# Moving the first B load to ScalarE's hardware queue, beside the first A load, in a one-core matmul and logsumexp kernel

## The chip, the core and the metric

The kernel runs on one core of one Trainium2 chip. The metric is the device time of one launch in microseconds (us). Executions of one kernel differ by about 2 us, so an effect of half a microsecond needs medians and intervals. Engine names in the profile: PE is the TensorE matmul, PEld its weight load, DVE is VectorE, ACT is ScalarE, POOL is GpSimd, SP is SyncE. A trailing "q" (SPq, ACTq) is the engine's sequencer, which issues transfers.

## The reference

```python
m, k, n = 1024, 4096, 4096
def reference(a, b):                      # float32, normal random
    x = np.matmul(a, b)
    return special.logsumexp(x, axis=-1).astype(np.float32)
```

## The kernel before

A and B come from DRAM as float32 and are worked on as float16. The product over the first 512 columns of B is done plainly, while A arrives and is transposed on TensorE; later blocks use a seven-product scheme that is not touched here. In that first stage, up to about 58 us, GpSimd's software queue brings 128x512 tiles of A and pairs of B rows, and casts them in the transfer. Only the very first tile of A (raw_a, 256 KB) and the first pair of B rows (raw_b, 512 KB) come as float32 by a hardware queue, and are cast by engines, because that queue starts earlier (first packets at 1.76 us, the software queue's at 3.97, in before's trace).

```python
    # ScalarE's activation tables, first thing in the program      [cut: set_id]
    nc.scalar.add_instruction(mybir.InstLoadActFuncSet(...))
    ...
    zeros = s5[:, KP - 1].rearrange("p q c -> p (q c)")
    nc.vector.memset(zeros[:, 0:FD], 0.0)
    warm(6)                               # six useless matmuls, to raise TensorE's clock
    coming = list(arrivals)

    def first(k0, kn, what, x):
        if what == "a":
            raw = fix_pool.tile([P, FD], f32, name="raw_a", tag="e")
            ...
            nc.sync.dma_start(out=raw, in_=a_m[x, :, k0 * P : (k0 + kn) * P])
            nc.vector.tensor_copy(out=slot, in_=raw)
            stg[k0, x] = slot
        else:
            raw = fix_pool.tile([P, 2, FD], f32, name="raw_b", tag="s")
            nc.sync.dma_start(out=raw, in_=b_rows[:, 0, :, 0:FD])
            nc.vector.tensor_copy(out=blk0.raw[0][:, 0, 0], in_=raw[:, 0])
            nc.scalar.copy(out=blk0.raw[0][:, 0, 1], in_=raw[:, 1])

    def load(k0, kn, what, x):            # loads run ahead by up to 12 tiles
        if len(coming) >= len(arrivals) - 2:
            first(k0, kn, what, x)
        elif what == "a":
            load_a(k0, kn, x)             # nc.gpsimd.dma_start
        else:
            blk0.load(k0 // 2, k0 // 2 + 1)   # nc.gpsimd.dma_start
        ...
    for n, (k0, kn, what, x) in enumerate(arrivals):
        ...
        if what == "a":
            transpose_group(k0, kn, x)    # 4 transposes, then one copy out of PSUM
        if k0 < KN and x < 3:
            warm(1)
        ...                               # the products of what has arrived
```

GpSimd's transfers use eight semaphores in turn, so its ninth transfer waits until its first has landed, and so on.

## Time and profile before

| | before |
|---|---|
| median of 6 runs | 421.9 us (421.21 to 423.07) |
| span in the profiled run | 420.3 us |
| first real matmul starts at | 5.96 us |
| TensorE busy, 15.5 to 82 us | 66.43 of 66.50 us |

From the profile's page, the chain of work that ended last, by engine:

```profile
PE 97%; DMA 1%; DVE 0%; ACT 0%; issue 0%; SPq 0%; ACTq 0%
```

The start is in the timeline. Columns: start and length in us, engine, line, operation, output and inputs, count; in brackets, how long the engine had been idle and what ended that.

```profile
0.74 1.28 ACT L56 ACT_TABLE_LOAD   x1 [0.74 <-PEq L592]
0.75 0.39 SPq L295 DMA_DIRECT2D raw_a<-in_a_dram  x1
1.20 2.74 PE L282 MATMUL acc_1_96<-s_73 128*128 128x512 f16 x6 [1.20 <-DVE s_73 L285]
1.20 0.41 SPq L300 DMA_DIRECT2D raw_b<-in_b_dram  x1
3.46 0.52 DVE L296 CAST tb<-raw_a 128x512 f16<-128x512 f32 x1 [2.32 <-DMA raw_a<-in_a_dram]
4.04 0.61 PE L203 MATMUL tps_97<-ident,tb 128*128 128x128 f16 x4
5.07 0.52 DVE L301 CAST b_0_83<-raw_b 128x512 f16<-128x512 f32 x1 [1.09 <-DMA raw_b<-in_b_dram]
5.50 0.40 DVE L214 COPY aT<-tps_97 128x512 f16<-128x512 f16 x1
5.96 1.03 PE L221 MATMUL acc_0_91<-b_0_83,aT 128*128 128x512 f16 x2 [0.47 <-DVE aT L214]
```

SyncE issues raw_a at 0.75 and raw_b at 1.20. VectorE casts raw_a when it lands, TensorE transposes it at 4.04, and VectorE could copy the transposes out at about 4.7. It stands in line behind its cast of raw_b, though, which lands only at 5.04. So the first real matmul waits for raw_b.

The DMA view, first for the stretch from 2.5 to 4.0 us (queue: packets, MB, share of the 16 engines' time; q1 is SyncE's hardware queue), then the two issues (size, us from issue to landing):

```profile
q1 hardware_dynamic: 300, 0.58, 102.3%
...
raw_b<-in_b_dram SPq DMA_DIRECT2D x1, 512.0 KB, 3.8
raw_a<-in_a_dram SPq DMA_DIRECT2D x1, 256.0 KB, 2.7
```

A share can exceed 100%, as here. One queue keeps the 16 engines at 102% and moves 0.58 MB in 1.5 us, or 385 GB/s.

### The profile page before, as it was taken

The page shows a single profiled execution, that of the slowest core. Times are in us where ns is not written, and L with a number is a line of the kernel's source. Part 1 is how long each engine was busy: PE and PEld are TensorE (multiplying, and loading weights), DVE is VectorE, ACT ScalarE, POOL GpSimd, SP SyncE. Part 2 cuts the span into 40 slices and gives each one's busy share as a digit, 9 for nine tenths or more (in the row PEclk, how much of TensorE's full clock was granted, in tenths as well). Part 3 has the DMA queues.
Part 4 walks back from the last instruction along what each step waited for, and adds up shares of the span by engine and source line. Part 5 has one row for each costly group of instructions (what it writes and reads, how often), then busy time and mean ns, then how long its engine had stood idle before and what let it go on. Part 6 is the DMA issues. An engine that isn't in the chain of part 4 may idle for free.

```text
span 420.3 us, 8528 instructions
## 1 busy us (share of the span) xinstructions
PE 414.1 (99%) x3643; PEld 348.7 (83%) x3643; DVE 259.4 (62%) x573; ACT 109.8 (26%) x279; POOL 73.0 (17%) x115
## 2 busy tenths in 40 slices
PE   8999999999999999999999999999999999999995
PEld 3555558888888888888888888888888888888885
DVE  2567587978657783258722694336832587299855
ACT  2222240141132222122222212222221222222124
POOL 7676753001010120003000030001200030120000
PEclk9999999999999999999999999999999999999999
DMA  9999999999999299003990079400990039899000
GB/s 185 202 203 203 202 205 207 207 207 214 176 199 201 39 186 207 9 2 45 207 151 2 2 123 207 73 2 2 189 207 6 2 59 207 136 188 207 8 2 1
DMA packets 57845, 53.37 MB, mean 127 GB/s; under 512 B 10192, under 2 KB 56912, under 8 KB 57808
## 3 DMA queue, kind: packets, MB, share of 16 engines
q0 software_dynamic: 48928, 49.95, 72.1%
q1 hardware_dynamic: 8880, 2.89, 4.0%
q8 instruction: 28, 0.46, 0.4%
q14 instruction: 9, 0.07, 0.0%
HBM read 100.66 MB, written 2.10 MB: 245 GB/s over the span
## 4 chain that ended last, share of the span: by engine, by line
PE 97%; DMA 1%; DVE 0%; ACT 0%; issue 0%; SPq 0%; ACTq 0%
PE acc_1_92 L221 2%; PE acc_0_91 L221 2%; PE acc_0_93 L221 2%; PE acc_1_0_1343 L399 2%; PE acc_1_0_765 L399 2%; PE acc_2_0_3643 L399 2%; PE acc_2_0_767 L399 2%; PE acc_1_0_2435 L399 2%; PE acc_0_0_763 L399 2%; PE acc_2_0_4199 L399 2%; PE acc_3_0_3231 L399 2%; PE acc_0_0_2847 L399 2%; PE acc_3_0_1611 L399 2%; PE acc_2_0_1478 L399 2%; PE acc_0_0_3927 L399 2%; PE acc_1_0_2975 L399 2%
## 5 line engine op out<-in xcount | busy, mean ns | idle before, releaser
L399 PEld LDWEIGHTS <-aT 128*128 128x128 f16 x1856 | 181.5, 98 | 21.3
L399 PEld LDWEIGHTS <-s_71 128*128 128x128 f16 x464 | 45.3, 98 | 5.5
L399 PEld LDWEIGHTS <-s_73 128*128 128x128 f16 x464 | 45.4, 98 | 5.3
L399 PEld LDWEIGHTS <-s_72 128*128 128x128 f16 x464 | 45.4, 98 | 5.3
L221 PEld LDWEIGHTS <-aT 128*128 128x128 f16 x192 | 16.8, 99 | 15.0 <-DVE aT L214 1.6
L192 POOL DMA_DIRECT2D tb<-in_a_dram x47 | 25.4, 543 | 8.1 <-DMA tb<-in_a_dram 3.1
L203 PEld LDWEIGHTS <-tb 128*128 128x128 f16 x192 | 15.0, 99 | 12.3 <-DVE tb L296 1.0
L216 ACT COPY aT<-tps_98 128x512 f16<-128x512 f16 x24 | 14.0, 585 | 38.7 <-PE tps_98 L203 38.7
L214 DVE COPY aT<-tps_97 128x512 f16<-128x512 f16 x24 | 10.2, 424 | 19.3 <-PE tps_97 L203 19.3
L84 DVE TENSOR_TENSOR aT<-aT 128x256 f16<-128x256 f16 (+1 forms) x56 | 16.1, 342 | 0.0
L203 PE MATMUL tps_97<-ident,tb 128*128 128x128 f16 x96 | 9.5, 223 | 0.1
L81 DVE TENSOR_TENSOR s_71<-aT 128x256 f16<-128x256 f16 (+1 forms) x26 | 8.2, 315 | 2.2 <-ACT aT L216 2.2
L203 PE MATMUL tps_98<-ident,tb 128*128 128x128 f16 x96 | 9.5, 224 | 0.0
L138 POOL DMA_DIRECT2D b_0_2299<-in_b_dram x1 | 0.9, 878 | 45.9 <-PE acc_3_0_2151 L399 45.9
L138 POOL DMA_DIRECT2D b_0_3379<-in_b_dram x1 | 0.9, 878 | 45.7 <-PE acc_3_0_3231 L399 45.7
L138 POOL DMA_DIRECT2D b_0_3919<-in_b_dram x1 | 0.9, 878 | 45.1 <-PE acc_3_0_3771 L399 45.1
L138 POOL DMA_DIRECT2D b_0_2839<-in_b_dram x1 | 0.9, 887 | 44.9 <-PE acc_3_0_2691 L399 44.9
L81 DVE TENSOR_TENSOR s_73<-aT 128x256 f16<-128x256 f16 (+1 forms) x26 | 8.2, 316 | 0.0
L81 DVE TENSOR_TENSOR s_72<-aT 128x256 f16<-128x256 f16 (+1 forms) x26 | 8.2, 316 | 0.0
L138 POOL DMA_DIRECT2D aT<-in_b_dram x4 | 3.5, 897 | 21.5 <-PE acc_1_0_4055 L399 21.5
L282 PE MATMUL acc_1_96<-s_73 128*128 128x512 f16 x11 | 5.2, 609 | 1.2 <-DVE s_73 L285 1.2
L81 DVE TENSOR_TENSOR tb<-aT 128x1024 f16<-128x1024 f16 x8 | 5.2, 687 | 1.5 <-DMA aT<-in_b_dram 1.5
(1050 smaller groups left out, 893.0 us busy)
## 6 DMA issues: line engine op xcount, KB each, us to landing
tb<-in_a_dram POOLq DMA_DIRECT2D x47, 128.0 KB, 5.9
aT<-in_b_dram POOLq DMA_DIRECT2D x4, 1024.0 KB, 15.2
b_1_84<-in_b_dram POOLq DMA_DIRECT2D x4, 256.0 KB, 6.2
b_2_85<-in_b_dram POOLq DMA_DIRECT2D x4, 256.0 KB, 6.2
b_3_86<-in_b_dram POOLq DMA_DIRECT2D x4, 256.0 KB, 6.2
b_0_87<-in_b_dram POOLq DMA_DIRECT2D x2, 512.0 KB, 8.6
b_1_88<-in_b_dram POOLq DMA_DIRECT2D x2, 512.0 KB, 11.8
b_2_89<-in_b_dram POOLq DMA_DIRECT2D x2, 512.0 KB, 15.2
```

The source lines that it names most:

```text
L81: nc.vector.tensor_tensor(out=o, in0=x, in1=y, op=ALU.add)
L84: nc.vector.tensor_tensor(out=o, in0=x, in1=y, op=ALU.subtract)
L138: nc.gpsimd.dma_start(out=self.raw[lo // GI][:, lo % GI : lo % GI + hi - lo], in_=b_rows[:, lo:hi, :, ts(self.nb, FD)],)
L192: nc.gpsimd.dma_start(out=slot, in_=a_m[m, :, k0 * P : (k0 + kn) * P])
L203: nc.tensor.matmul(pst[:, ts(j, P)], src[:, ts(j, P)], ident, is_transpose=True, start=(j == 0), stop=(j == kn - 1),)
L214: nc.vector.tensor_copy(out=dst, in_=v)
L216: nc.scalar.copy(out=dst, in_=v)
L221: nc.tensor.matmul(pt, aT[:, i, kp, m // 2, m % 2, :], blk0.raw[i // GI][:, i % GI, kp, :], start=(done[m] == 0), stop=(done[m] == KT - 1),)
L282: nc.tensor.matmul(acc[2][1], zeros[:, 0:P], zeros[:, 0:FD], start=True, stop=True)
L399: nc.tensor.matmul(c, lhs(i), rhs(i), start=(start and i == 0), stop=(i == KP - 1), skip_group_check=True,)
```

## The change

raw_b is to start with raw_a instead of behind it: it goes to ScalarE's hardware queue, and its issue is put ahead of ScalarE's table load. The instruction orders of TensorE, VectorE and GpSimd are the same in both kernels.

```diff
-    tables = list(get_activation_tables(nc.m.arch).items())
-    ...
-    nc.scalar.add_instruction(mybir.InstLoadActFuncSet(...))
     ...
     warm(6)
 
+    raw_a = fix_pool.tile([P, FD], f32, name="raw_a", tag="e")
+    raw_b = fix_pool.tile([P, 2, FD], f32, name="raw_b", tag="s")
+    nc.scalar.dma_start(out=raw_b, in_=b_rows[:, 0, :, 0:FD])
+    nc.sync.dma_start(out=raw_a, in_=a_m[0, :, 0 : KN * P])
+    tables = list(get_activation_tables(nc.m.arch).items())
+    ...
+    nc.scalar.add_instruction(mybir.InstLoadActFuncSet(...))
+
     coming = list(arrivals)
     ...                      # first(): the two dma_start are gone, the casts stay
```

## The prediction

> **What bounds the kernel.** The chain of waits is 97% TensorE and 1% DMA; from 15.5 to 82 us TensorE is busy 66.43 of 66.50 us (table of stretches). So a shift of the first real matmul should pass through to the end nearly one for one. The change touches only the first 6 us (chain in order of time): SyncE issues raw_b at 1.20, behind raw_a; it lands at 5.04; VectorE casts half of it until 5.58; behind that, in order, it copies the first transposes; the first real matmul starts at 5.96. TensorE is idle 0.47 us before that and about 0.1 us at 3.94.
>
> **What the change does.** The instruction orders of TensorE, VectorE and GpSimd stay the same. SyncE loses one issue (0.41 us), ScalarE gets it, and its table load (1.28 us) moves from 0.74 to about 1.15-2.45; ScalarE waits for raw_b until 5.07, so the load stays hidden. raw_b's issue moves 0.45 us forward: naive gain 0.45 us.
>
> **Why I expect less.** The DMA engines limit the two transfers, not the issue. On the hardware queue 786 KB move between about 1.9 and 4.4 us; from 2.5 to 4.0 its packets take 98 to 105% of the 16 engines, at about 390 GB/s (DMA view). raw_b follows raw_a without a hole. The Trainium skill, "DMA: Bandwidth & Descriptors", section "Issuing engines are not separate DMA queues", says such transfers interleave on the same 16 engines and only issue time is saved; the full engines in the trace agree. I estimate that raw_b lands at 4.7-5.0 (2.0-2.5 us was filled to 74% only, and less of its tail would meet the software queue that starts at 3.9).
> raw_a pays: with packets alternating, its 128 end after some 256 of 384 instead of first. Estimate from 2.4 us for all: 0.6-0.8 us later, landing at 4.0-4.2 instead of 3.43. Then cast 0.52, transposes, copy. Before, the copy could have started at about 4.7 had VectorE been free; it started at 5.58. With raw_a at 4.1 it can start at about 5.35-5.45, with raw_b's cast done at 5.25-5.5. First real matmul at 5.8-5.95: a gain of 0-0.2 us. Both inputs become critical together.
>
> **Second-order: the clock.** Matmuls of 512 columns take 0.43 us until about 9.4 and 0.22 after (timeline). The Trainium skill, "TensorE: Matmul & The Clock Gate", Part 1, says full clock follows about 3.4 us of sustained activity in free-running windows. The change moves TensorE's gap: 0.7-0.8 us idle after the six warm-up matmuls, then none before the first real matmul. The late unbroken run starts earlier, but the early one, from 1.2 to 5.5, is lost. This shifts single runs by up to some 1.5 us (before's runs spread 1.9 us); on average I put it at zero.
>
> **Prediction.** 421.7 us, 8 in 10 within 420.7 to 422.7. Faster by over 2%: 0.5%; within 2%: 99%; slower by over 2%: 0.5%.
>
> **What would show it.** Right: raw_a lands 0.5 us or more later and raw_b under 0.35 us earlier although issued at about 0.75; hardware queues full between 2.5 and 4; VectorE's first cast at about 4.1; first real matmul at 5.8-5.95; TensorE idle before the first transposes; the rest shifted as a block. Wrong: raw_a still at 3.4 and raw_b at 4.6 (queues don't compete; first matmul at 5.5), or raw_b slower on ScalarE's queue.
>
> **What would make it wrong.** The clock rising one window (3.4 us) earlier or later in most runs: up to 1.7 us either way. Or a slow first use of ScalarE's queue.

## The result, and the profile after

| | before | after |
|---|---|---|
| median, all runs of this comparison | 421.72 us (20 runs) | 422.39 us (10 runs) |
| ratio of fast runs, 95% interval | | 1.0014 (1.0004 to 1.0023) |
| span in the profiled run | 420.3 us | 421.8 us |
| raw_a issued / its cast starts | 0.75 / 3.46 | 0.74 / 4.47 |
| raw_b issued / its casts start | 1.20 / 5.07 | 0.74 / 5.62 |
| first real matmul | 5.96 us | 6.49 us |

A ratio is the mean time of one kernel's fast runs over that of the other's in the same rounds, so it is not quite the ratio of the medians. Here it says about 0.6 us slower: small, but the interval leaves out 1. The profiled run of after took 423.61 us, more than any of its ten timed runs, so its trace shows an uncommonly large loss; a second trace is given below.

The timeline of after, for the lines shown of before:

```profile
0.74 0.46 ACTq L278 DMA_DIRECT2D raw_b<-in_b_dram  x1
0.74 0.39 SPq L279 DMA_DIRECT2D raw_a<-in_a_dram  x1
1.19 2.74 PE L270 MATMUL acc_1_95<-s_72 128*128 128x512 f16 x6 [1.19 <-DVE s_72 L273]
1.23 1.28 ACT L283 ACT_TABLE_LOAD   x1 [1.23 <-PEq L592]
4.47 0.58 DVE L298 CAST tb<-raw_a 128x512 f16<-128x512 f32 x1 [3.33 <-DMA raw_a<-in_a_dram]
5.10 0.61 PE L191 MATMUL tps_96<-ident,tb 128*128 128x128 f16 x4 [1.17 <-DVE tb L298]
5.62 0.48 DVE L301 CAST b_0_82<-raw_b 128x512 f16<-128x512 f32 x1 [0.57 <-DMA raw_b<-in_b_dram]
6.03 0.41 DVE L202 COPY aT<-tps_96 128x512 f16<-128x512 f16 x1
6.49 1.03 PE L209 MATMUL acc_0_90<-b_0_82,aT 128*128 128x512 f16 x2
```

Both transfers are issued at 0.74, as intended, and both land later than before: raw_a by 1.0 us, and raw_b by 0.55 us although it was issued 0.46 us earlier. TensorE is idle for 1.17 us before the first transposes. The DMA view of the same stretch and issues (q10 is ScalarE's hardware queue):

```profile
q10 hardware_dynamic: 122, 0.25, 59.0%
q1 hardware_dynamic: 96, 0.17, 38.1%
...
raw_b<-in_b_dram ACTq DMA_DIRECT2D x1, 512.0 KB, 4.9
raw_a<-in_a_dram SPq DMA_DIRECT2D x1, 256.0 KB, 3.7
```

Read the two columns against each other. The shares add up to 97%, nearly what they were, yet the two queues together moved 0.42 MB where one had moved 0.58. A busy engine isn't a full one: the packets took longer each (97% over 218 packets is about 107 ns each, 102% over 300 about 82).

The loss doesn't end there. The hardware transfers now reach further into the time of the software queue. Two lines of GpSimd's timeline, its issue of the third software pair of B, in before and in after; it waits for its second transfer to land:

```profile
7.77 0.71 POOL L138 DMA_DIRECT2D b_0_83<-in_b_dram  x1 [0.65 <-DMA b_0_83<-in_b_dram]
```

```profile
9.12 0.71 POOL L126 DMA_DIRECT2D b_0_82<-in_b_dram  x1 [2.01 <-DMA b_0_82<-in_b_dram]
```

That second transfer landed at 7.48 before and at 8.84 after (from the traces' semaphore records), and everything behind it in the queue is late. The chain of waits of after, in order of time (start, us, what), now runs through such transfers, and meets TensorE at 23.55:

```profile
2.45 6.39 DMA b_0_82<-in_b_dram
...
9.12 6.18 DMA b_0_82<-in_b_dram
...
16.47 7.04 DMA tb<-in_a_dram
23.55 0.40 PE tps_96 L191 x4
```

The same group of transposes in TensorE's timeline, before and then after:

```profile
22.47 0.39 PE L203 MATMUL tps_97<-ident,tb 128*128 128x128 f16 x4
```

```profile
23.55 0.40 PE L191 MATMUL tps_96<-ident,tb 128*128 128x128 f16 x4 [0.59 <-DMA tb<-in_a_dram]
```

I compared the start of each of the 48 transpose groups in the two traces. After lags by 0.52 us at the second group, by 0.34 from the third on (below), and then by 0.90, 1.02 and 1.50 after three places where TensorE waits for a tile. 1.5 us is the whole difference of the two spans.

Why 0.52 becomes 0.34: TensorE's clock rose to full at 9.46 us in before and at 9.61 in after (the traces' clock records; in the timeline, matmuls of 512 columns stop taking 0.43 us each). The work between the first matmul and that moment goes at half speed, so a late start loses about half of its delay. Here that is 0.26, and the clock's own 0.15 later costs half of that again, 0.08: together 0.34.

The software queue had no room to give. From 24 to 41 us of before it moves 203 GB/s at 123% of the engines' nominal time, and from the 32nd software tile on many land only 0.2 to 0.3 us before TensorE uses them, 0.17 at the least. So TensorE is busy all the time and the tile stream is full all the time: the stage has two limits, side by side, and the chain of waits of before shows only one.

### The profile page after: what moved, and what is told of

Read it like the earlier page. It is cut to its first block, busy times and chain, and to the rows that moved or that the text cites. A ratio compares the mean times of both kernels' runs of the same rounds, so it can differ in the third digit from the quotient of the medians.

```text
span 421.8 us, 8528 instructions
## 1 busy us (share of the span) xinstructions
PE 414.1 (98%) x3643; PEld 347.9 (82%) x3643; DVE 259.4 (62%) x573; ACT 109.8 (26%) x279; POOL 73.0 (17%) x115
## 4 chain that ended last, share of the span: by engine, by line
PE 92%; DMA 6%; issue 1%; POOL 0%; ACT 0%; DVE 0%; POOLq 0%; ACTq 0%
DMA tb<-in_a_dram 3%; DMA b_0_82<-in_b_dram 3%; PE acc_1_0_1343 L399 2%; PE acc_1_0_765 L399 2%; PE acc_1_0_1895 L399 2%; PE acc_2_0_767 L399 2%; PE acc_3_0_2691 L399 2%; PE acc_2_0_4199 L399 2%; PE acc_3_0_3771 L399 2%; PE acc_0_0_2307 L399 2%; PE acc_2_0_1478 L399 2%; PE acc_1_0_4055 L399 2%; PE acc_3_0_3231 L399 2%; PE acc_2_0_3103 L399 2%; PE acc_2_0_2563 L399 2%; PE acc_0_0_1767 L399 2%
```

## The experiments

The rivals for the late transfers: **T**, the table load right behind ScalarE's issue holds its queue back until the load ends at 2.5 us (the queue's first packet came at 2.63). **Q**, ScalarE's queue is slow in itself. **S**, two hardware transfers that start together get less than one after the other. For the time: **P**, only the first matmul's delay counts; **D**, the delay of the software queue costs by itself.

Eleven runs followed; all gave correct results (after_again is the changed kernel once more). "Hardware MB" is what both hardware queues had started to move by 4.0 us (DMA view); the clock is the moment when the trace's record shows full speed; the casts' starts stand for the landings.

| kernel | raw_a cast | raw_b cast | hardware MB by 4.0 | first matmul | clock full at | span | ratio to before (95%) |
|---|---|---|---|---|---|---|---|
| before | 3.46 | 5.07 | 0.73 | 5.96 | 9.46 | 420.3 | |
| after | 4.47 | 5.62 | 0.51 | 6.49 | 9.61 | 421.8 | 1.0014 (1.0004 to 1.0023) |
| after_again | 4.39 | 5.43 | 0.59 | 6.25 | 9.65 | 420.7 | 1.0006 (0.9988 to 1.0023) |
| table_waits | 4.27 | 5.42 | 0.59 | 6.24 | 10.08 | 421.5 | 1.0017 (1.0004 to 1.0030) |
| swapped | 4.52 | 5.42 | 0.55 | 6.23 | 4.43 | 420.5 | 1.0019 (1.0005 to 1.0034) |
| table_first | 3.87 | 5.14 | 0.65 | 6.10 | 9.71 | slow | 1.0016 (1.0003 to 1.0029) |
| both_on_act | 3.63 | 4.91 | 0.72 | 5.73 | 5.00 | 419.8 | 1.0001 (0.9985 to 1.0018) |
| b_act_later | 3.80 | 5.09 | 0.69 | 6.03 | 4.40 | 420.6 | 0.9999 (0.9987 to 1.0011) |
| pool_late | 3.62 | 4.90 | 0.69 | 5.86 | 5.27 | 419.9 | 1.0001 (0.9987 to 1.0014) |
| dve_late | 3.67 | 4.96 | 0.69 | 6.63 | 9.51 | 420.7 | 1.0006 (0.9994 to 1.0019) |
| extra_hw | 3.72 | 5.00 | 0.71 | 5.96 | 10.14 | 420.8 | 1.0023 (1.0007 to 1.0040) |
| split_b | 3.41 | 4.31, 6.95 | 0.53 | 5.13 | 4.58 | 421.7 | 1.0007 (0.9992 to 1.0023) |
| copy_first | 3.56 | 4.99 | 0.70 | 5.63 | 5.21 | 420.3 | 0.9999 (0.9981 to 1.0016) |

### table_waits: no table load near the transfers

```diff
-    nc.sync.dma_start(out=raw_a, ...)
+    dma_a = nc.sync.dma_start(out=raw_a, ...)
     ...
+    tc.add_manual_dep(load_ins, dma_a.ins.name, <sync, data>)   # table load waits for raw_a
```

> The changed kernel, with ScalarE's table load made to wait until raw_a has landed (about 4.4 us), so that no table load runs while the two transfers start. Theory S (two hardware queues side by side share what makes or fetches their descriptors, and get less together than one queue alone): nothing changes, raw_b's first packet stays near 2.6 us, raw_a lands near 4.4, raw_b near 5.5. Theory T (the table load right behind ScalarE's issue holds back its queue until the load ends at 2.5): raw_b's first packet comes at about 1.8, and both have landed by about 5.0. The late load itself delays ScalarE's cast of raw_b to about 5.8 in both, so the time may be up to 0.3 us above the changed kernel's.

The timeline of table_waits, its issue of raw_b and its table load:

```profile
0.73 0.46 ACTq L278 DMA_DIRECT2D raw_b<-in_b_dram  x1
4.26 1.28 ACT L283 ACT_TABLE_LOAD   x1 [4.26 <-DMA raw_a<-in_a_dram]
```

The DMA view from 0 to 2.5 us, of table_waits (q1 carries raw_a, q10 raw_b):

```profile
q1 hardware_dynamic: 49, 0.10, 23.9%
q10 hardware_dynamic: 1, 0.00, 0.2%
```

The load now runs at 4.26 to 5.54, and ScalarE's queue still starts only at the end of that window: its first packet came at 2.48. Both landings stay late. Theory T falls.

### both_on_act: one queue, but ScalarE's

```diff
-    nc.scalar.dma_start(out=raw_b, ...)
-    nc.sync.dma_start(out=raw_a, ...)
+    nc.scalar.dma_start(out=raw_a, ...)
+    nc.scalar.dma_start(out=raw_b, ...)
```

> Both transfers on ScalarE's hardware queue, raw_a first, ahead of the table load; SyncE's queue unused. Theory S (sharing): one queue alone again, so as the kernel before: raw_a first packet at 1.75, lands near 3.4, raw_b near 5.0, time that of the kernel before within 0.2 us. Theory T (table load holds the queue back): nothing moves before the load ends at about 2.9, raw_a lands near 4.5. Theory Q (ScalarE's queue is slow in itself): raw_a's first packet at about 2.6, lands past 4.

The DMA view of both_on_act from 0 to 2.5 us:

```profile
q10 hardware_dynamic: 79, 0.16, 25.9%
```

On ScalarE's queue alone, 0.16 MB had moved by 2.5 us (before 0.16, after 0.10), raw_a and raw_b land as in before, and the time is before's. Theory Q falls.

### swapped: raw_a on ScalarE's queue, raw_b on SyncE's

```diff
-    nc.scalar.dma_start(out=raw_b, ...)
-    nc.sync.dma_start(out=raw_a, ...)
+    nc.sync.dma_start(out=raw_b, ...)
+    nc.scalar.dma_start(out=raw_a, ...)
```

> The changed kernel with the queues exchanged: raw_a on ScalarE's, raw_b on SyncE's. Theory Q or T (something about ScalarE's queue): raw_a's first packet at about 2.6, lands at 4.2 to 4.6, raw_b by 4.6 to 5.0. Theory S, if it is symmetric: raw_a's first packet near 1.75 and raw_b's late. In both raw_a lands later than 3.9 and the time is no better than the changed kernel's, 422.2 to 423.

raw_a's first packet came at 1.78, now from ScalarE's queue, and raw_b's at 2.51, now from SyncE's. So the delay of 0.7 us belongs to raw_b in every such run, not to a queue: against T and Q, for S. Both land late as in after, and the time is 0.8 us (0.19%) above before's. Why it was raw_a each time the runs don't tell; its issue was the shorter of the two.

### table_first: the table load back in front

```diff
+    <table load>
     nc.scalar.dma_start(out=raw_b, ...)
     nc.sync.dma_start(out=raw_a, ...)
-    <table load>
```

> The changed kernel with the table load back in front of ScalarE's issue, so that raw_b is issued at about 2.0 us, when raw_a's descriptors are already out. Theory S: raw_a has its start to itself, first packet 1.75, lands near 3.4 to 3.6; raw_b's first packet near 3.0, lands at 5.5 to 5.7; first real matmul near 6.5. Theory T: the same first packet of raw_b about 1.0 us after its issue. If raw_a still lands past 4 with raw_b issued so late, S in its form 'at the start only' is wrong and the sharing is one of packets. Time 422.0 to 422.6.

Its timeline, the table load and the two issues:

```profile
0.73 1.28 ACT L281 ACT_TABLE_LOAD   x1 [0.73 <-PEq L592]
0.74 0.39 SPq L290 DMA_DIRECT2D raw_a<-in_a_dram  x1
0.77 0.44 ACTq L289 DMA_DIRECT2D raw_b<-in_b_dram  x1
```

The expectation's premise failed: ScalarE issued raw_b at 0.77, while its table load was running, not behind it at 2.0. "Ahead of the table load" was worth 0.03 us. So this run is nearly the changed kernel, and its ratio, 1.0016, is the same. Its profile: slow (a granted clock of 0.755, 543 us), so its span isn't compared; of its transfers I only note that they were late by less (raw_a landed at 3.84, and 0.65 MB had started by 4.0 us), so a common start doesn't always cost the same. SyncE's issue began 0.02 us before ScalarE's here; in the other four runs with a common start ScalarE's came first, by under 0.01. Whether that matters isn't tested.

### b_act_later: ScalarE's queue, issued as late as in before

```diff
-    nc.vector.memset(zeros[:, 0:FD], 0.0)
+    filled = nc.vector.memset(zeros[:, 0:FD], 0.0)
     ...
-    nc.scalar.dma_start(out=raw_b, ...)
+    dma_b = nc.scalar.dma_start(out=raw_b, ...)
+    tc.add_manual_dep(dma_b.ins, filled.ins.name, <sync, data>)   # raw_b issued at 1.17
```

> The changed kernel, with ScalarE's issue of raw_b made to wait for VectorE's first memset, so that it comes at about 1.2 us, when SyncE issued it before; only the queue differs from the kernel before. Theory G1 (only a start at the same time hurts, in whatever prepares the transfers): raw_a lands at 3.4 to 3.7, raw_b at 4.9 to 5.2, time as before's within 0.2 us. Theory G2 (packets of two hardware queues alternate and get less together than those of one queue, whatever the start): raw_a lands at 3.9 or later, raw_b at 5.2 or later, time 0.3 us or more above before's.

Its timeline, the issue of raw_b and VectorE's casts of raw_a and raw_b:

```profile
1.17 0.43 ACTq L278 DMA_DIRECT2D raw_b<-in_b_dram  x1
3.80 0.43 DVE L304 CAST tb<-raw_a 128x512 f16<-128x512 f32 x1 [2.66 <-DMA raw_a<-in_a_dram]
5.09 0.56 DVE L307 CAST b<-raw_b 128x512 f16<-128x512 f32 x1 [0.86 <-DMA raw_b<-in_b_dram]
```

This separates the queue from the moment. With the issue held back to 1.17 us, the two queues are as good as one: raw_b lands at 5.06, earlier than when it was issued at 0.74, raw_a at 3.77, between what G1 and what G2 expected, and the time is before's (0.9999). The form G1 of theory S fits better: it is the start at the same time that costs. But this is one trace, and its two queues overlap only from 2.69 to 3.33 us (raw_b's first packet to raw_a's last; in after from 2.63 to 3.96), so a loss that grows with the overlap, a milder G2, isn't excluded. It isn't clean in another respect: in this trace the second software transfer landed at 8.09, though the hardware queues were done early.

### after_again: the changed kernel once more

No edit.

> The changed kernel again, for a second trace and more times. Simultaneous issue as the cause: at most 300 of the 384 hardware packets have started by 4.0 us (before 358; with ScalarE's issue delayed to 1.17 us 335), raw_a lands at 4.2 to 4.5, raw_b at 5.3 to 5.6; slower than before by 0.3 to 0.9 us. If raw_a lands at 3.4 to 3.8 here, the first trace was an exception.

The transfers repeat the first trace in the main (0.59 MB by 4.0 us, landings at 4.37 and 5.41); its median is 422.45 us against 421.74. By the ratio that is 0.25 us, less than the 0.3 to 0.9 expected, and the interval of these five runs alone includes 1. In this trace the second software transfer landed at 7.74 and TensorE hardly waited for a tile: the lag is 0.24 us from the third transpose group on, and 0.35 at the end. So the late start is in both traces, and the waits for tiles differ between them, 0.1 and 1.2 us.

### pool_late: only the software queue later

```diff
+    for _ in range(4):
+        nc.gpsimd.memset(scratch, 0.0)
     back = []                          # the loop of loads follows
```

> The kernel before, with four small memsets on GpSimd ahead of its first load, so that the whole software queue starts about 0.5 to 0.9 us later while both hardware transfers stay as they were. Theory D (the changed kernel loses time because its hardware transfers end later and push back the software queue, whose tiles TensorE then has to wait for): the first real matmul stays near 5.96, the second software transfer lands near 8.1 to 8.4 instead of 7.48, and the time rises by 0.3 to 0.7 us. Theory P (it loses time because the first real matmul is late): the time stays within 0.2 us of before's.

Inconclusive. The memsets took 0.99 us, but only the first software transfer was clearly late (6.38 instead of 5.88); the second landed at 7.66 instead of 7.48. From 5 to 7.5 us of before the software queue takes 121% of the engines' nominal time, so they probably set its pace, and not GpSimd's issues. The edit didn't push the queue back, and the time, 1.0001, tells nothing on D.

The trace shows something else, though. Its DMA view for SyncE's queue, from 0 to 2.5 us and from 2.5 to 4.0:

```profile
q1 hardware_dynamic: 51, 0.10, 25.6%
q1 hardware_dynamic: 302, 0.59, 104.4%
```

The one queue began as slowly here as two queues do after a common start (after 47 packets by 2.5 us, after_again 53). Yet it then moved 0.59 MB (after 0.42, after_again 0.48), and raw_a landed at 3.59. So a slow beginning by itself costs little.

### dve_late: only the first matmul later

```diff
             nc.vector.tensor_copy(out=blk0.raw[0][:, 0, 0], in_=raw[:, 0])
+            for _ in range(4):
+                nc.vector.memset(scratch, 0.0)
```

> The kernel before, with four small memsets on VectorE between its cast of raw_b and its copy of the first transposes, so that the first real matmul starts at about 6.5 as in the changed kernel, while no transfer moves. Theory P: the time rises by 0.25 us (a delay of 0.5 at half clock) to 0.5 us. Theory D: it rises by less than 0.2 us, since the tiles come when they came before and the later work is paced by them.

The first real matmul in its timeline:

```profile
6.63 1.03 PE L222 MATMUL acc<-b,aT 128*128 128x512 f16 x2 [1.02 <-DVE aT L215]
```

The first matmul starts 0.67 us later, and from the third transpose group to the last the trace lags by an even 0.37: no tile is waited for, so nothing gives it back or adds to it. The spans differ by 0.4. The timed runs, 1.0006, are in accord with 0.37 us (0.09%) but can't tell it from nothing. So in this trace P is right as far as it goes: the late start passes on at about half, which was D's miss.

### extra_hw: the hardware queue busy longer, the first matmul where it was

```diff
             nc.sync.dma_start(out=raw, in_=b_rows[:, 0, :, 0:FD])
+            spare = dram_pool.tile([P, FD], f32, name="spare")
+            nc.sync.dma_start(out=spare, in_=a_m[1, :, 0:FD])     # read by nothing
```

> The kernel before, with a third, useless transfer of 256 KB (from DRAM to DRAM) on SyncE's queue behind raw_b, so that the hardware queue keeps the engines for longer while the software queue is already running. Raw_a and raw_b should land as before (3.4 to 3.7, 4.9 to 5.1) and the first real matmul start at about 5.9. Theory D (a software queue pushed back costs time by itself): the second software transfer lands 0.6 us or more later than 7.48 and the time rises by 0.3 to 0.7 us. Theory P (only the first matmul counts): time within 0.2 us of before's.

Its first real matmul, GpSimd's wait at the issue shown of before and after, and the third transpose group (10.06 in before):

```profile
5.96 1.04 PE L221 MATMUL acc<-b,aT 128*128 128x512 f16 x2 [0.30 <-DVE aT L214]
8.52 0.71 POOL L138 DMA_DIRECT2D b<-in_b_dram  x1 [1.41 <-DMA b<-in_b_dram]
10.40 0.39 PE L203 MATMUL tps<-ident,tb 128*128 128x128 f16 x4
```

The first matmul starts at 5.96, as in before; the second software transfer lands at 8.24, 0.75 later; and the time is 1.0023, about 1.0 us more, clear of noise and above the 0.3 to 0.7 that D expected. So P alone falls: 256 KB more in front of the tile stream cost time with TensorE's start untouched.

D isn't shown by this, though. The profiled run was the fastest of the five, and its span is only 0.5 us longer than before's. Of that lag 0.34 is there at the third transpose group, ahead of any wait for a tile: it is half of the clock's later rise (10.14 against 9.46). Waits for tiles add 0.20. And this kernel moves 256 KB that the changed kernel doesn't: at the 203 GB/s of the full stream they take some 1.3 us, as an estimate. Nor does a late second software transfer settle it: in b_act_later it landed at 8.09, and the time was before's.

### copy_first: an earlier first matmul, with the loads of before

```diff
-            nc.vector.tensor_copy(out=blk0.raw[0][:, 0, 0], in_=raw[:, 0])
-            nc.scalar.copy(out=blk0.raw[0][:, 0, 1], in_=raw[:, 1])
+            casts.append(raw)
     ...
             transpose_group(k0, kn, x)
+            <the two casts, once, behind the first group's copy>
```

> The kernel before with two instructions exchanged on VectorE: it copies the first transposes out, which are ready at about 4.7, before it casts raw_b, which lands at about 5.0. The first real matmul should start at about 5.6 instead of 5.96. Theory P: faster by 0.15 to 0.35 us. Theory D, or a stage paced by the tile stream: faster by at most 0.15 us, within noise.

The waits of TensorE (what waited for what: us in total, times, longest):

```profile
PE tps L203 <- DMA tb<-in_a_dram: 1.5, 3, 0.8
PE acc L282 <- DVE s L285: 1.2, 1, 1.2
```

The first matmul starts at 5.63, 0.33 earlier, and the clock also rose early, at 5.21, so TensorE led before's trace by 1.63 us at the eighth transpose group. Then it waited 1.5 us for tiles and ended the stage 0.02 behind. The time is 0.9999. The tile stream takes a lead back, as it does in the other traces with an early clock: both_on_act led by 1.52 and kept 0.52, and swapped led by 1.01 and ended 0.18 behind.

### split_b: raw_b in two halves on one queue

```diff
-            nc.sync.dma_start(out=raw, in_=b_rows[:, 0, :, 0:FD])
+            for t in range(2):
+                nc.sync.dma_start(out=raw[:, t], in_=b_rows[:, 0, t, 0:FD])
```

> The kernel before, with raw_b's load cut in two on SyncE's queue, one for each half that is cast by itself, so that VectorE's cast needn't wait for ScalarE's half. The first half should land near 4.3 and the first real matmul start at 5.2 to 5.4 instead of 5.96; the second half lands near 5.0 as before, the software queue stays as it was. Theory P: faster by 0.3 to 0.6 us. Theory D: faster by 0.2 us or less, as the stage ends when the tile stream does.

The second real matmul, which needs the second half, in its timeline:

```profile
7.62 0.38 PE L221 MATMUL acc<-b,aT 128*128 128x512 f16 x1 [2.10 <-ACT b L303]
```

The first half came as expected and the first matmul started at 5.13, but the second half landed at 6.93, not near 5.0, and TensorE stood for 2.10 us in between. In this trace the clock even fell back to half from 8.00 to 11.41. The time shows no gain. The hardware MB by 4.0 us, 0.53, are as low as with a common start, here from one queue. The software queue's first packet came at 3.34 here, ahead of the second half's last ones; why the third hardware transfer fares so badly is open.

## Why the prediction was right or wrong

- **Time.** 422.39 lies in the range of 420.7 to 422.7, and within 2%. The direction inside the range was wrong: it predicted the first matmul 0 to 0.2 us earlier; it came 0.53 later, and the kernel is about 0.6 us slower. That the time fell in the range is owed to the range's width, 1 us to either side, and says nothing for the mechanism.
- **The naive gain of 0.45 us isn't there.** Right in that: raw_b was issued 0.46 us earlier and this bought nothing.
- **raw_a pays.** Right in kind, small in size: 4.0 to 4.2 was predicted, and it landed at 4.45 and 4.37.
- **"I estimate that raw_b lands at 4.7-5.0".** This step failed: 5.60 and 5.41. The estimate took the 2.4 us for all 786 KB from before's trace as fixed. I had taken from the skill only that the transfers interleave and that issue time is saved. Starting together lowered the rate itself: 0.51 and 0.59 MB by 4.0 us instead of 0.73. The prediction's own sign against it, "raw_b slower on ScalarE's queue", came up, but both_on_act, swapped and table_waits show that neither the queue nor the table load is the reason; with b_act_later that leaves the common start. Beneath that, the cause is only argued. The Trainium skill, "Perfetto Trace Analysis", section "DMA Instruction — HWDGE (DVE, Sync)", says that the block which generates the descriptors is shared between sequencers (it names those of VectorE and SyncE), and "DMA: Bandwidth & Descriptors", section "Queues, rings and completion order", says that SyncE and ScalarE have no generator of their own. It would fit that raw_b's packets come only from 2.3 to 2.6 us on, in the five traces with a common start. But no run shows the block itself, and three things speak against it as the whole story. The two issues, side by side, don't show a wait for each other (0.46 and 0.39 us; in before, one after the other, 0.41 and 0.39). raw_a's slow beginning (47 packets instead of 77 by 2.5 us) cost little in pool_late (raw_a landed at 3.59, in before at 3.44). And of the 0.22 MB that after lacks by 4.0 us, 0.16 are lost after 2.5 us, with the engines 97% busy on longer packets. Why a common start costs stays open.
- **"Hardware queues full between 2.5 and 4".** It came out as predicted, 97%, and was no sign of what I meant: the bytes were 0.42 MB instead of 0.58. The sign should have been in MB.
- **"A shift of the first real matmul should pass through to the end nearly one for one."** This failed twice. At half clock a late start costs about half (0.53 gave 0.34, of which 0.08 is the clock's; 0.67 gave 0.37 in dve_late). And the stage is limited by the tile stream as well, so a lead of TensorE's is taken back (copy_first), and the shift isn't a block: in after's first trace it grows from 0.34 to 1.5 us. That a later stream costs by itself is likely from there, but not shown (extra_hw also moves more bytes). In after's first trace the waits for tiles were 1.2 of the 1.5 us, in the second 0.1 of 0.35. How the average of 0.6 us divides between late start and tile waits isn't settled.
- **The clock.** Some runs' clock rises early and others' a good 4 us later: right. The traces are too few to say whether an edit shifts the side: of the five with a common start four rose late, of the eight others three. If the common start does shift it, that is part of the 0.6 us; no run tests this rival. "Up to some 1.5 us" for a run was too much: the traces with an early clock span 419.8 to 420.6 us (without split_b, whose clock fell back), so they gain at most about 0.5 on before, since the tile stream takes most of the lead back.
- **The table load.** It stays hidden, as predicted, and it never mattered: table_first issues raw_b at 0.77 anyway.

No version here beats before. By their ratios both_on_act, b_act_later, pool_late and copy_first equal it to 0.01%, with intervals of 0.1 to 0.2% to either side.

## What to carry to other kernels

If two loads are needed in order, issue them in order: putting them side by side at the program's start cost both of them here. Read a queue's MB beside its busy share, since a share near 100% hid over a quarter of the rate here (0.42 MB against 0.58). And where an engine is busy for 99% of a stage, still look how long before its use each input lands; here a margin of 0.2 us meant that there were two limits, and that a gain on one of them was mostly taken back by the other.

## What the Trainium skill lacked or had wrong

- "DMA: Bandwidth & Descriptors", "Issuing engines are not separate DMA queues": it says that issuing from several engines at once only saves issue time. Here it cost: 0.51 to 0.65 MB moved by 4.0 us in the five traces with a common start, 0.69 to 0.73 in the six with both loads on one queue (raw_b in one piece), 0.69 from two queues 0.43 us apart.
- "TensorE: Matmul & The Clock Gate", Part 1: it puts the rise to full clock about 4 us into sustained activity, within 500 ns from run to run. Warm-up matmuls began at 1.2 us here. In six of thirteen traces the clock rose at 4.40 to 5.27, so 3.2 to 4.1 us later, about as it says, and in seven at 9.46 to 10.14, with short gaps in TensorE's work between (0.1 to 1.2 us). As the page speaks of sustained activity, this doesn't contradict it; but gaps as short stand before an early rise too (0.2 us in both_on_act), so these traces don't tell what decides.
- "DMA: Bandwidth & Descriptors", "Specifications": about 0.6 us to the first byte by a hardware queue. The first packet came at 1.74 to 1.78 in these traces, so 1.0 us after the issue's start and 0.6 after its end in before (1.14). For the software queue it says about 1 us; with the hardware queues busy, its first packet came at 3.97 in before and 4.24 in after, 2.1 us and more after the end of the first issue (1.91); in split_b at 3.34, 1.4 us after it.
- "ScalarE: Activation LUTs", "What ACT_TABLE_LOAD costs": 1283 ns for the load agrees (1.28 us). No page says that ScalarE's sequencer issues a transfer while the load is running: issue at 0.77, load from 0.73 to 2.01.
